# Segment mean over ten million sorted values: 90 rows of 875 in place of 98 rows of 800, looks from sums of probes, tables eight wide

## The chip, the core and the metric

The kernel runs on one core of a Trainium2 chip. The metric is the time of the whole program on the device in microseconds. The profile is one execution taken by the hardware profiler; its span runs from the first to the last instruction, and its own time is a little longer than the span.

## The reference: what is computed

```
data:        10,000,000 float32
segment_ids: 10,000,000 int64, sorted, 10,000 segments
sums[s]   = sum of data where segment_ids == s
counts[s] = number of elements where segment_ids == s
out[s]    = sums[s] / max(counts[s], 1)
```

The ids are sorted draws, so a segment is a run of about 1,000 neighbouring elements; in the fixed draw the shortest has 886 elements and the longest 1,136.

## The kernel before, in words

**Tiling.** Each of the 128 partitions owns D = 78,125 neighbouring elements, cut into NR = 98 rows of L = 800 (the last has 525). A row of one partition holds at most one boundary between segments, because a segment is longer than a row. The kernel doesn't read all ids. It finds each boundary in two looks.

**First look.** *Probes* are every S = 160th id, five to a row, one packet of 8 bytes each; `load_probes` (L153) loads them on SP's queue in 20 groups of four or five rows. `first_look` (L230 to L285) works on VectorE on one group: ten small operations compare the probes of a row with the first, add up how many are equal (`jc`), work out the place of the interval that holds the boundary (`ST`, `pos`, `IDX`) and a constant for the second look (`QQ`), and the boundary count of the row (`BT`) and its complement (`NB`). A row without exactly one boundary gets an index beyond the array.

**Second look.** `gather` (L287) is an indirect DMA on POOL's queue for each row; it fetches W = 159 ids for every partition into one of RING = 28 slots of `GT`, and nothing for partitions whose index is out of bounds. `add_ids` (L298) adds them on ScalarE; since the ids take only two values, the sum tells where the boundary is. `second_look` (L304) subtracts it from `QQ` and gives `KK`, the boundary's place within the row.

**Data.** `load_data` (L157) brings two rows a tile, 800 KB in a DMA of SP's queue, into 18 buffers. `total` (L310) sums a row on ScalarE into `T`. `split` (L316, the instruction at L319) sums on VectorE what lies ahead of the boundary: a ramp in PSUM is compared with `KK`, multiplied by the data and summed into `A`. `T - A` belongs to the next segment (`B`).

**Putting segments together.** A segment can start in one row and end in a later one, or in the next partition. `counts` (L521) carries the places of boundaries through rows by a scan and takes reciprocals of the lengths; `sums` (L560) does so for the partial sums (`FF`). `extend` (L372) shifts the first E = 24 rows of every partition to the partition below by a matmul, and `ext_rows` (L579) handles these. `select`, `table` (L633, L640) move results from row order to segment order: `windows` (L368) lets four neighbouring outputs look at the same twelve rows, compares keys with the output's number (`sel`), multiplies by the results and adds up (`tab`). `place` (L654, its second call on POOL) moves each partition's table to its place among the 79 outputs of a partition, by thirteen shifts (`shf`). The last outputs aren't taken from the table: `pick` (L672) prepares weights from the last rows, two wide operations of it on POOL, and `all_but_last` and `finish` (L696, L710) use them when the last sums are there. `check`, `check_late` and `verdict` (L450 to L519) make sure that the windows hold; if not, `general_path` computes everything in another way.

**Order.** It is written by hand. The loop over rows at the end issues, for each row r, loads up to X_DATA = 26 rows ahead and probes 13 further, `add_ids` of row r + 6, then `total` and `split` of row r, then whatever `put` has hung behind that row: looks 11 rows ahead of their group, `counts`, `sums`, `table` and so on at rows chosen by hand. Each engine and each DMA queue takes its instructions in this order and waits for what it needs.

Of the kernel before, what the change touches and what calls it, by code (L numbers as in the profile page):

```python
# [9 lines left out]
FP32 = mybir.dt.float32  # L10
BF16 = mybir.dt.bfloat16
I32 = mybir.dt.int32
# [7 lines left out]
L = 800  # L20
S = 160
K = L // S
NR = 98
LAST = D - (NR - 1) * L
W = S - 1
E = 24
NX = NR + E
BIG = float(1 << 24)
GROUPS = [4] + [5] * 18 + [4]
X_PROBE = 13  # L30
X_DATA = 26
X_LOOK = 11
X_SUM = 6
RING = 28
# [3 lines left out]
NT1 = 92  # L38
R1 = 84
R2 = NR + 4  # L40
C1 = 50
# [71 lines left out]
def kernel(  # L113
# [30 lines left out]
    NPR = (D + S - 1) // S  # L144

# [20 lines left out]

    wb_i = cpool.tile([P, NR], I32, name="wb_i")
    wb = cpool.tile([P, NR], FP32, name="wb")
    nc.gpsimd.iota(wb_i, pattern=[[L, NR]], base=-W, channel_multiplier=D)  # L169
# [3 lines left out]
    nc.gpsimd.iota(i_i, pattern=[[1, L]], base=0, channel_multiplier=0)  # L173
# [3 lines left out]
    nc.gpsimd.iota(rp_i[:, 0:NR], pattern=[[L, NR]], base=0, channel_multiplier=0)  # L177
    nc.gpsimd.iota(rp_i[:, NR:NX], pattern=[[L, E]], base=D, channel_multiplier=0)
# [3 lines left out]
    nc.gpsimd.iota(ur_i, pattern=[[1, NX]], base=0, channel_multiplier=0)  # L182
    nc.vector.tensor_scalar(out=ur, in0=ur_i, scalar1=-1.625, scalar2=None, op0=ALU.add)
# [24 lines left out]
    jj_i = cpool.tile([P, NT1], I32, name="jj_i")  # L208
    jj = cpool.tile([P, NT1], FP32, name="jj")
    nc.gpsimd.iota(jj_i, pattern=[[1, NT1]], base=0, channel_multiplier=0)  # L210
# [3 lines left out]
    PAD = 2  # L214
    q5 = cpool.tile([P, 5, NX + PAD], FP32, name="q5")
    nc.vector.memset(q5, 0.0)
    V, BT, KK, A, B = (q5[:, i, PAD:] for i in range(5))
    vend = cpool.tile([P, 1], FP32, name="vend")
    ST = cpool.tile([P, NR], FP32, name="ST")
    IDX = cpool.tile([P, NR], I32, name="IDX")  # L220
    QQ = cpool.tile([P, NR], FP32, name="QQ")
    GS = cpool.tile([P, NR], FP32, name="GS")
    T = cpool.tile([P, NR], FP32, name="T")
    NB = cpool.tile([P, NX], FP32, name="NB")
    GT = gpool.tile([P, RING, W], I64, name="GT")
    gt32 = GT.bitcast(I32)
# [3 lines left out]
    def first_look(g):  # L230

        a, b = bounds[g], bounds[g + 1]
        n = b - a
        eq = fpool.tile([P, n, K - 1], FP32, name="eq", bufs=3)
        jc = fpool.tile([P, n], FP32, name="jc", bufs=3)
        pos = fpool.tile([P, n], FP32, name="pos", bufs=3)
        last = b == NR

        def s1():
            if last:  # L240
                nc.vector.tensor_copy(out=pr32[:, NR - 1, 2 * (K - 1) : 2 * K], in_=snt32)
                nc.vector.tensor_copy(out=vend, in_=snt32[:, 0:1])
                nc.vector.tensor_copy(out=V[:, NR : NR + 1], in_=snt32[:, 0:1])
            in1b, in0b = bass.broadcast_tensor_aps(pr32[:, a:b, 0:1], pr32[:, a:b, 2 : 2 * K : 2])
            nc.vector.tensor_tensor(out=eq, in0=in0b, in1=in1b, op=ALU.is_equal)  # L245
            e = b if last else b + 1
            nc.vector.tensor_copy(out=V[:, a:e], in_=pr32[:, a:e, 0])  # L247

        def s2():
            nc.vector.tensor_reduce(out=jc, in_=eq, axis=AX.X, op=ALU.add)  # L250
            nc.vector.tensor_sub(out=BT[:, a:b], in0=V[:, a + 1 : b + 1], in1=V[:, a:b])  # L251

        def s3():
            nc.vector.tensor_scalar(  # L254
                out=ST[:, a:b], in0=jc, scalar1=float(S), scalar2=float(1 + W),
                op0=ALU.mult, op1=ALU.add,
            )
            nc.vector.tensor_scalar(  # L258
                out=NB[:, a:b], in0=BT[:, a:b], scalar1=1.0, scalar2=None, op0=ALU.not_equal
            )  # L260
            if last:
                nc.vector.tensor_scalar(
                    out=ST[:, NR - 1 : NR], in0=ST[:, NR - 1 : NR], scalar1=float(LAST), scalar2=None,
                    op0=ALU.min,
                )

        def s4():
            nc.vector.tensor_add(out=pos, in0=ST[:, a:b], in1=wb[:, a:b])  # L268
            nc.vector.scalar_tensor_tensor(  # L269
                out=QQ[:, a:b], in0=V[:, a:b], scalar=float(W), in1=ST[:, a:b],  # L270
                op0=ALU.mult, op1=ALU.add,
            )

        def s5():
            nc.vector.scalar_tensor_tensor(  # L275
                out=IDX[:, a:b], in0=NB[:, a:b], scalar=BIG, in1=pos, op0=ALU.mult, op1=ALU.add
            )

            nc.vector.scalar_tensor_tensor(  # L279
                out=QQ[:, a:b], in0=NB[:, a:b], scalar=-64.0 * BIG, in1=QQ[:, a:b], op0=ALU.mult,  # L280
                op1=ALU.add,
            )
            gather(g)

        return [s1, s2, s3, s4, s5]  # L285
# [12 lines left out]
    def add_ids(r):  # L298
        nc.scalar.activation(  # L299
            out=junk_a[:, 0:W], in_=gt32[:, r % RING, 0 : 2 * W : 2], func=ACT.Relu,  # L300
            accum_out=GS[:, r : r + 1],
        )

    def second_look(a, b):  # L304
        def s1():
            nc.vector.tensor_sub(out=KK[:, a:b], in0=QQ[:, a:b], in1=GS[:, a:b])  # L306

        return [s1]
# [23 lines left out]
    CS = cpool.tile([P, R2 + 1], FP32, name="CS")  # L332
    CX = cpool.tile([P, E + 1], FP32, name="CX")
# [3 lines left out]
    FF = cpool.tile([P, NX], FP32, name="FF")  # L337
    RF = cpool.tile([P, NX + PAD], FP32, name="RF")
    sel = cpool.tile([P, NT1 // 4, 4, 12], FP32, name="sel")
    tab = cpool.tile([P, NT1], FP32, name="tab")  # L340
    shf = cpool.tile([P, NO, ND], FP32, name="shf")
    KL = cpool.tile([P, R2 - R1], FP32, name="KL")
    pk = cpool.tile([P, NO - C1, R2 - R1], FP32, name="pk")
# [6 lines left out]
    nc.vector.memset(CS[:, 0:1], 0.0)  # L350
    nc.vector.memset(CX[:, 0:1], 0.0)
# [3 lines left out]
    MID = 68  # L355
    NBAD = 2 * (NR - MID) + 2
    bad0 = cpool.tile([P, 2 * (MID + E) + 5], FP32, name="bad0")
    bad = cpool.tile([P, NBAD], FP32, name="bad")
    vx = cpool.tile([P, 1], FP32, name="vx")
    bads = cpool.tile([P, 1], FP32, name="bads")  # L360
# [4 lines left out]
    def view(ap, dims):  # L365
        return bass.AP(ap.tensor, ap.offset, [list(ap.ap[0])] + dims)

    def windows(ap, m0, m1):  # L368

        return view(ap[:, 5 * m0 : 5 * m0 + 1], [[5, m1 - m0], [0, 4], [1, 12]])  # L370

    def extend():  # L372

        def s1():
            nc.vector.tensor_sub(out=B[:, 0:E], in0=T[:, 0:E], in1=A[:, 0:E])

# [23 lines left out]
    def keys(a, b):  # L400
        def s1():
            if a == 0:
                nc.vector.tensor_add(out=base1, in0=V[:, 0:1], in1=pin)

        def s2():
            nc.vector.tensor_scalar(
                out=KEY[:, PAD + a : PAD + b], in0=V[:, a:b], scalar1=base1[:, 0:1], scalar2=None,
                op0=ALU.subtract,
            )
            if a == 0:  # L410
                nc.vector.tensor_sub(out=delta, in0=sp, in1=base1)

        def s3():
            if a == 0:
# [6 lines left out]
    j1 = cpool.tile([P, NX], FP32, name="j1")  # L421
# [417 lines left out]
```

## Time and profile before

| | |
|---|---|
| time, median of 5 runs | 195.54 us (194.1 to 197.33) |
| time of the profiled execution | 195.72 us |
| its span | 194.0 us |
| VectorE (DVE) busy | 148.5 us, 77% of the span, 551 instructions |
| ScalarE (ACT) busy | 138.2 us, 71%, 393 instructions |
| POOL busy | 104.9 us, 54%, 117 instructions |
| `split`, L319 | 98 instructions, 102.3 us, mean 1,044 ns |
| `total`, L314 | 98 instructions, 85.0 us, mean 867 ns |
| `add_ids`, L299 | 98 instructions, 33.9 us, mean 346 ns |
| gathers, L289 | 98 instructions, 98.0 us, mean 1,000 ns |
| DMA | 53.40 MB in 75,141 packets, 65,601 of them under 512 B |

How to read it: the page gives each engine's busy time, then the span in 40 slices (a digit is the busy share in tenths), then the DMA queues with packets, MB and the share that their packets took of 16 engines' span, then the chain that ended last and the costliest groups of instructions. An answer of order in time gives start, duration, engine, line, operation and the tiles, with the idle time before it and what ended that. VectorE is DVE there, ScalarE ACT, SyncE SP; the queue of an engine has a q behind its name.

### The profile page before, as it was taken

Reading aid. Unit: us, or ns where it says so; the run is one execution under the profiler, and the core shown is the slowest. Engines: PE = TensorE matmul, PEld = TensorE weight load, DVE = VectorE, ACT = ScalarE, POOL = GpSimd, SP = SyncE. Lnnn points to the kernel's source line nnn. Section 1 sums busy time; section 2 is a strip of 40 time slices with the busy share of each in tenths; the row PEclk is TensorE's granted clock in tenths of the full one; section 3 lists DMA queues with packets and bytes.
Section 4 is the critical chain, followed back from the end, with each engine's and each line's share of the span. In section 5 each row is a group of like instructions: output and inputs, shape, how many; then the busy total and the mean of one; then the engine's idle time right before and its main releaser. Section 6 shows DMA issues by size and latency. Waiting matters only on the chain.

```text
span 194.0 us, 1611 instructions
## 1 busy us (share of the span) xinstructions
PE 1.6 (1%) x6; PEld 1.4 (1%) x6; DVE 148.5 (77%) x551; ACT 138.2 (71%) x393; POOL 104.9 (54%) x117
## 2 busy tenths in 40 slices
PE   0000000000000100000000000000000000001000
PEld 0000000000001000000000000000000000001000
DVE  6533596988694939596797949797998688999991
ACT  0221798999997869596869868687867697987800
POOL 5487765766657372846546472847275654762000
DMA  5999999999999999999999999899999999993000
GB/s 63 135 168 350 280 401 228 303 349 353 293 250 393 244 337 216 408 212 376 279 380 245 271 360 296 258 247 408 236 361 273 396 266 413 402 397 153 2 0 10
DMA packets 75141, 53.40 MB, mean 275 GB/s; under 512 B 65601, under 2 KB 65684, under 8 KB 75127
## 3 DMA queue, kind: packets, MB, share of 16 engines
q1 hardware_dynamic: 70251, 40.54, 74.5%
q0 software_dynamic: 4704, 12.74, 22.6%
q14 instruction: 14, 0.11, 0.2%
q10 hardware_dynamic: 172, 0.00, 0.1%
HBM read 56.46 MB, written 0.04 MB: 291 GB/s over the span
## 4 chain that ended last, share of the span: by engine, by line
DMA 41%; SPq 29%; DVE 13%; issue 9%; POOL 3%; ACT 2%; POOLq 0%; ACTq 0%; DVEq 0%
DMA data_t<-in_data_dram 34%; SPq L161 24%; DMA GT<-in_segment_ids_dram,IDX 8%; DVE junk_v L319 6%; SPq L153 5%; POOL GT L289 3%; ACT junk_a L314 1%; ACT junk_a L299 1%; DVE FF L572 1%; DVE most L706 0%; DVE pk L684 0%; DVE add L701 0%; DVE sel L642 0%; DVE sel L628 0%; DVE tab L647 0%
## 5 line engine op out<-in xcount | busy, mean ns | idle before, releaser
L289 POOL DMA_INDIRECT GT<-in_segment_ids_dram,IDX x98 | 98.0, 1000 | 67.1 <-ACT junk_a L299 24.1
L319 DVE SCALAR_TENSOR_TENSOR junk_v<-iota,q,data_t 128x800 bf16<-128x800 f32 x98 | 102.3, 1044 | 25.5 <-DMA data_t<-in_data_dram 23.7
L314 ACT ACTIVATE junk_a<-data_t 128x800 bf16<-128x800 f32 x98 | 85.0, 867 | 14.3 <-DMA data_t<-in_data_dram 11.3
L299 ACT ACTIVATE junk_a<-GT 128x159 bf16<-128x159 int32 x98 | 33.9, 346 | 23.8 <-DMA GT<-in_segment_ids_dram,IDX 19.3
L299 ACT ACTIVATION_READ_ACCUMULATOR junk_a<-GT 128x1 f32 x98 | 18.3, 187 | 0.0
L314 ACT ACTIVATION_READ_ACCUMULATOR junk_a<-data_t 128x1 f32 x98 | 18.3, 186 | 0.0
L306 DVE TENSOR_TENSOR q<-QQ,GS 128x5 f32<-128x5 f32 (+1 forms) x20 | 3.2, 160 | 7.3 <-ACT junk_a L299 3.9
L319 DVE DVE_READ_ACCUMULATOR junk_v<-iota,q,data_t 128x1 f32 x98 | 8.1, 82 | 0.0
L245 DVE TENSOR_TENSOR eq<-pr 128x20 f32<-128x20 int32 (+1 forms) x20 | 3.4, 172 | 4.6 <-issue 2.5
L299 ACT ACT_TABLE_LOAD x1 | 1.3, 1283 | 7.6 <-DMA data_t<-in_data_dram 7.6
L254 DVE TENSOR_SCALAR ST<-jc 128x5 f32<-128x5 f32 (+1 forms) x20 | 3.8, 192 | 0.0
L268 DVE TENSOR_TENSOR pos<-ST,wb 128x5 f32<-128x5 f32 (+1 forms) x20 | 3.3, 166 | 0.5 <-DVE NB L258 0.4
L275 DVE SCALAR_TENSOR_TENSOR IDX<-NB,pos 128x5 int32<-128x5 f32 (+1 forms) x20 | 3.3, 164 | 0.5 <-DVE QQ L269 0.5
L250 DVE TENSOR_REDUCE jc<-eq 128x5 f32<-128x20 f32 (+1 forms) x20 | 3.5, 175 | 0.0
L258 DVE TENSOR_SCALAR NB<-q 128x5 f32<-128x5 f32 (+1 forms) x20 | 3.5, 174 | 0.0
L247 DVE CAST q<-pr 128x6 f32<-128x6 int32 (+2 forms) x20 | 3.3, 166 | 0.0
L279 DVE SCALAR_TENSOR_TENSOR QQ<-NB,QQ 128x5 f32<-128x5 f32 (+1 forms) x20 | 3.2, 162 | 0.0
L269 DVE SCALAR_TENSOR_TENSOR QQ<-q,ST 128x5 f32<-128x5 f32 (+1 forms) x20 | 3.1, 157 | 0.0
L251 DVE TENSOR_TENSOR q<-q 128x5 f32<-128x5 f32 (+1 forms) x20 | 3.1, 155 | 0.0
L657 POOL TENSOR_TENSOR shf<-tab,dm 128x559 f32<-128x559 f32 x1 | 1.3, 1331 | 1.9 <-DVE tab L647 1.9
L647 DVE TENSOR_REDUCE tab<-sel 128x32 f32<-128x384 f32 (+2 forms) x3 | 1.6, 531 | 0.0
L170 DVE CAST wb<-wb_i 128x98 f32<-128x98 int32 x1 | 0.8, 783 | 1.1 <-POOL wb_i L169 1.1
(107 smaller groups left out, 42.1 us busy)
## 6 DMA issues: line engine op xcount, KB each, us to landing
data_t<-in_data_dram SPq DMA_DIRECT2D x48, 800.0 KB
GT<-in_segment_ids_dram,IDX POOLq DMA_INDIRECT x98
pr<-in_segment_ids_dram SPq DMA_DIRECT2D x18, 25.0 KB
data_t<-in_data_dram SPq DMA_DIRECT2D x1, 400.0 KB
data_t<-in_data_dram SPq DMA_DIRECT2D x1, 262.5 KB
out_dram<-OUT SPq DMA_DIRECT2D x1, 36.6 KB
pr<-in_segment_ids_dram SPq DMA_DIRECT2D x1, 21.0 KB
pr<-in_segment_ids_dram SPq DMA_DIRECT2D x1, 18.0 KB
```

What stands on the lines that cost most here:

```text
L153: nc.sync.dma_start(out=pr_flat[:, a:b], in_=ids_p[:, a * S : (b - 1) * S + 1 : S])
L161: nc.sync.dma_start(out=d[:, 0 : c - a], in_=data_p[:, a:c])
L245: nc.vector.tensor_tensor(out=eq, in0=in0b, in1=in1b, op=ALU.is_equal)
L247: nc.vector.tensor_copy(out=V[:, a:e], in_=pr32[:, a:e, 0])
L250: nc.vector.tensor_reduce(out=jc, in_=eq, axis=AX.X, op=ALU.add)
L254: nc.vector.tensor_scalar(out=ST[:, a:b], in0=jc, scalar1=float(S), scalar2=float(1 + W), op0=ALU.mult, op1=ALU.add,)
L258: nc.vector.tensor_scalar(out=NB[:, a:b], in0=BT[:, a:b], scalar1=1.0, scalar2=None, op0=ALU.not_equal)
L268: nc.vector.tensor_add(out=pos, in0=ST[:, a:b], in1=wb[:, a:b])
L289: nc.gpsimd.indirect_dma_start(out=GT[:, r % RING, :], out_offset=None, in_=ids2d[:], in_offset=bass.IndirectOffsetOnAxis(ap=IDX[:, r : r ...
L299: nc.scalar.activation(out=junk_a[:, 0:W], in_=gt32[:, r % RING, 0 : 2 * W : 2], func=ACT.Relu, accum_out=GS[:, r : r + 1],)
L314: nc.scalar.activation(out=junk_a[:, 0:n], in_=d, func=ACT.Copy, accum_out=t)
L319: nc.vector.scalar_tensor_tensor(out=junk_v[:, 0:n], in0=iota[:, 0:n], scalar=KK[:, r : r + 1], in1=d, op0=ALU.is_lt, op1=ALU.mult, accum_ ...
```

## The change

- **Rows and probes.** Rows of 875 elements, 90 of them, the last with 250; a probe every 175 elements, still five to a row (447 in place of 489 for a partition). Groups are 15 of six rows. Gathers fetch 175 ids. The ring of `GT` has 20 slots, the tables for the next partition E = 20 rows. Looks go 12 rows ahead, probes 14, `add_ids` 7.
- **Looks.** `first_look` adds up the row's probes (`SG`) and takes `ST = 5 * next row's first id - SG`; with one boundary this is the number of probes behind it. Zero, no boundary, is sent out of bounds by adding 2^18 before the multiplication by 175. `YY` replaces `QQ`. `BT` and `NB` are made later, for many rows at once, in `keys`. `add_ids` uses a plain copy and no longer a ReLU, and ScalarE fills all of `GT` with zeros at the start.
- **Counts and sums.** The scans run on maxima and on sums with the multiplier of the row, so that fewer operations are needed; a row without a boundary is pushed far below by `-512 * FAR`.
- **Tables.** `windows` is eight rows wide and slides by one row for each output, seven outputs to eight rows. The part of the table that comes from the next partition has its own table (`tax`), placed early. All of `place` runs on VectorE; `pick` gets a third wide operation on POOL.
- **Check.** One check of all rows behind rows 74 to 76, its verdict behind rows 77 and 78.

```diff
-L = 800
-S = 160
+L = 875
+S = 175
 K = L // S
-NR = 98
+NR = 90
 LAST = D - (NR - 1) * L
-W = S - 1
-E = 24
+TAIL = LAST - S
+W = S
+E = 20
 NX = NR + E
-BIG = float(1 << 24)
-GROUPS = [4] + [5] * 18 + [4]
-X_PROBE = 13
+FAR = float(1 << 18)
+GROUPS = [6] * 15
+X_PROBE = 14
 X_DATA = 26
-X_LOOK = 11
-X_SUM = 6
-RING = 28
+X_LOOK = 12
+X_SUM = 7
+RING = 20
 NO = 79
 SHIFT = 6
 ND = 2 * SHIFT + 1
-NT1 = 92
-R1 = 84
+NT1 = 91
+M1 = 10
+R1 = 8 * M1 - 2
 R2 = NR + 4
-C1 = 50
+C1 = 51
...
+    GT = gpool.tile([P, RING, W], I64, name="GT")
+    gt32 = GT.bitcast(I32)
+
+    def view(ap, dims):
+        return bass.AP(ap.tensor, ap.offset, [list(ap.ap[0])] + dims)
+
+    nc.scalar.activation(
+        out=gt32[:, :, 0 : 2 * W : 2], in_=view(q5[:, 0, 0:1], [[0, RING], [0, W]]), func=ACT.Copy
...
-        pos = fpool.tile([P, n], FP32, name="pos", bufs=3)
+        far = fpool.tile([P, n], FP32, name="far", bufs=3)
         last = b == NR
 
         def s1():
+            v = nc.vector
             if last:
-                nc.vector.tensor_copy(out=pr32[:, NR - 1, 2 * (K - 1) : 2 * K], in_=snt32)
-                nc.vector.tensor_copy(out=vend, in_=snt32[:, 0:1])
-                nc.vector.tensor_copy(out=V[:, NR : NR + 1], in_=snt32[:, 0:1])
-            in1b, in0b = bass.broadcast_tensor_aps(pr32[:, a:b, 0:1], pr32[:, a:b, 2 : 2 * K : 2])
-            nc.vector.tensor_tensor(out=eq, in0=in0b, in1=in1b, op=ALU.is_equal)
-            e = b if last else b + 1
-            nc.vector.tensor_copy(out=V[:, a:e], in_=pr32[:, a:e, 0])
-
-        def s2():
-            nc.vector.tensor_reduce(out=jc, in_=eq, axis=AX.X, op=ALU.add)
-            nc.vector.tensor_sub(out=BT[:, a:b], in0=V[:, a + 1 : b + 1], in1=V[:, a:b])
-
-        def s3():
-            nc.vector.tensor_scalar(
-                out=ST[:, a:b], in0=jc, scalar1=float(S), scalar2=float(1 + W),
-                op0=ALU.mult, op1=ALU.add,
-            )
-            nc.vector.tensor_scalar(
-                out=NB[:, a:b], in0=BT[:, a:b], scalar1=1.0, scalar2=None, op0=ALU.not_equal
+                m = NR * K + 1 - NPR
+                v.tensor_copy(
+                    out=pr_flat.bitcast(I32)[:, 2 * NPR : 2 * (NPR + m)].rearrange("p (a b) -> p a b", b=2),
+                    in_=view(snt32[:, 0:1], [[0, m], [1, 2]]),
+                )
+            v.tensor_reduce(out=SG[:, a:b], in_=pr32[:, a:b, 0 : 2 * K : 2], axis=AX.X, op=ALU.add)
+            v.scalar_tensor_tensor(
+                out=ST[:, a:b], in0=VI[:, a + 1 : b + 1], scalar=float(K), in1=SG[:, a:b],
+                op0=ALU.mult, op1=ALU.subtract,
+            )
+            v.tensor_scalar(out=far, in0=ST[:, a:b], scalar1=0.0, scalar2=FAR, op0=ALU.is_equal, op1=ALU.mult)
+            v.tensor_add(out=ST[:, a:b], in0=ST[:, a:b], in1=far)
+            for c, d, w in [(a, b - 1, S), (b - 1, b, TAIL)] if last else [(a, b, S)]:
+                v.scalar_tensor_tensor(
+                    out=IDX[:, c:d], in0=ST[:, c:d], scalar=float(w), in1=wb[:, c:d], op0=ALU.mult, op1=ALU.add
+                )
+            v.scalar_tensor_tensor(
+                out=YY[:, a:b], in0=ST[:, a:b], scalar=float(K + 1), in1=SG[:, a:b], op0=ALU.mult, op1=ALU.add
             )
             if last:
-                nc.vector.tensor_scalar(
-                    out=ST[:, NR - 1 : NR], in0=ST[:, NR - 1 : NR], scalar1=float(LAST), scalar2=None,
-                    op0=ALU.min,
+                v.tensor_scalar(
+                    out=tl, in0=ST[:, NR - 1 : NR], scalar1=-1.0, scalar2=float(TAIL - S),
+                    op0=ALU.add, op1=ALU.mult,
                 )
-
-        def s4():
-            nc.vector.tensor_add(out=pos, in0=ST[:, a:b], in1=wb[:, a:b])
-            nc.vector.scalar_tensor_tensor(
-                out=QQ[:, a:b], in0=V[:, a:b], scalar=float(W), in1=ST[:, a:b],
-                op0=ALU.mult, op1=ALU.add,
-            )
-
-        def s5():
-            nc.vector.scalar_tensor_tensor(
-                out=IDX[:, a:b], in0=NB[:, a:b], scalar=BIG, in1=pos, op0=ALU.mult, op1=ALU.add
-            )
-
-            nc.vector.scalar_tensor_tensor(
-                out=QQ[:, a:b], in0=NB[:, a:b], scalar=-64.0 * BIG, in1=QQ[:, a:b], op0=ALU.mult,
-                op1=ALU.add,
-            )
             gather(g)
 
-        return [s1, s2, s3, s4, s5]
...
-            out=junk_a[:, 0:W], in_=gt32[:, r % RING, 0 : 2 * W : 2], func=ACT.Relu,
+            out=junk_a[:, 0:W], in_=gt32[:, r % RING, 0 : 2 * W : 2], func=ACT.Copy,
...
-            nc.vector.tensor_sub(out=KK[:, a:b], in0=QQ[:, a:b], in1=GS[:, a:b])
+            nc.vector.scalar_tensor_tensor(
+                out=KK[:, a:b], in0=YY[:, a:b], scalar=float(S // K), in1=GS[:, a:b],
+                op0=ALU.mult, op1=ALU.subtract,
...
+    nc.gpsimd.memset(tab, 0.0)
+    nc.gpsimd.memset(tax, 0.0)
+    nc.gpsimd.memset(shf[:, :, ND : ND + 1], 0.0)
+    nc.gpsimd.memset(add, 0.0)
...
-        return view(ap[:, 5 * m0 : 5 * m0 + 1], [[5, m1 - m0], [0, 4], [1, 12]])
+        return view(ap[:, 8 * m0 : 8 * m0 + 1], [[8, m1 - m0], [1, 7], [1, 8]])
...
+    def edges(a, b):
+        nc.vector.tensor_sub(out=BT[:, a:b], in0=VI[:, a + 1 : b + 1], in1=VI[:, a:b])
...
-    def counts(a, b):
+    def counts(a, b, mask=True):
 
 
         n = b - a
         ps = fpool.tile([P, n], FP32, name="ps")
-        bp = fpool.tile([P, n], FP32, name="bp")
         ct = fpool.tile([P, n], FP32, name="ct")
 
         def s1():
-            nc.vector.tensor_add(out=ps, in0=rp[:, a:b], in1=KK[:, a:b])
-
-        def s2():
-            nc.vector.tensor_mul(out=bp, in0=ps, in1=BT[:, a:b])
+            nc.vector.scalar_tensor_tensor(
+                out=ps, in0=NB[:, a:b], scalar=-512.0 * FAR, in1=KK[:, a:b], op0=ALU.mult, op1=ALU.add
+            )
+
+        def s2():
+            nc.vector.tensor_add(out=ps, in0=ps, in1=rp[:, a:b])
 
         def s3():
             nc.vector.tensor_tensor_scan(
-                out=PS[:, a + 1 : b + 1], data0=NB[:, a:b], data1=bp, initial=PS[:, a : a + 1],
-                op0=ALU.mult, op1=ALU.add,
+                out=PS[:, a + 1 : b + 1], data0=ps, data1=ps, initial=PS[:, a : a + 1],
+                op0=ALU.max, op1=ALU.max,
             )
 
         def s4():
             nc.vector.tensor_sub(out=ct, in0=ps, in1=PS[:, a:b])
 
         def s5():
-            nc.vector.tensor_scalar(out=ct, in0=ct, scalar1=1.0, scalar2=None, op0=ALU.max)
+            nc.vector.reciprocal(out=RB[:, a:b], in_=ct)
 
         def s6():
-            nc.vector.reciprocal(out=ct, in_=ct)
-
-        def s7():
-            c = min(b, NR)
-            nc.vector.tensor_mul(out=RB[:, a:c], in0=ct[:, 0 : c - a], in1=BT[:, a:c])
-            if b > NR:
-                nc.vector.tensor_mul(
-                    out=RB[:, NR:b], in0=ct[:, NR - a : n], in1=MX[:, 0 : b - NR]
-                )
-
-        return [s1, s2, s3, s4, s5, s6, s7]
+            nc.vector.tensor_mul(out=RB[:, a:b], in0=RB[:, a:b], in1=BT[:, a:b])
+
+        return [s1, s2, s3, s4, s5] + ([s6] if mask else [])
 
     def sums(a, b, weigh=True, upto=NR):
         def s1():
...
+            nc.vector.tensor_add(out=XX[:, a:b], in0=A[:, a:b], in1=q5[:, 4, PAD + a - 1 : PAD + b - 1])
+
+        def s3():
             nc.vector.tensor_tensor_scan(
-                out=CS[:, a + 1 : b + 1], data0=NB[:, a:b], data1=B[:, a:b], initial=CS[:, a : a + 1],
+                out=FF[:, a:b], data0=NBP[:, a:b], data1=XX[:, a:b], initial=FFP[:, a : a + 1],
                 op0=ALU.mult, op1=ALU.add,
             )
-
-        def s3():
-            nc.vector.tensor_add(out=FF[:, a:b], in0=A[:, a:b], in1=CS[:, a:b])
...
+    def place(c0, c1, t, outs):
+        def s1():
+            n = c1 - c0
+            nc.vector.tensor_tensor(
+                out=shf[:, c0:c1, 0:ND], in0=view(t[:, c0 : c0 + 1], [[1, n], [1, ND]]),
+                in1=view(dm[:, 0:1], [[0, n], [1, ND]]), op=ALU.mult,
+            )
+
+        def s2():
+            for a, b, d, o in outs:
+                nc.vector.tensor_reduce(out=o, in_=shf[:, a:b, 0:d], axis=AX.X, op=ALU.add)
+
+        return [s1, s2]
+
...
-                  view(jj[:, C1 : C1 + 1], [[1, n], [0, m]]))
+                out=pk, in0=view(KL[:, 0:1], [[0, n], [1, m]]), in1=view(jj[:, C1 : C1 + 1], [[1, n], [0, m]]),
+                op=ALU.subtract,
+            )
+            e.tensor_scalar(out=pk, in0=pk, scalar1=0.0, scalar2=None, op0=ALU.is_equal)
+            e.tensor_copy(out=BM[:, 0 : NR - R1], in_=BT[:, R1:NR])
+            e.tensor_copy(out=BM[:, NR - R1 : m], in_=MX[:, 0 : R2 - NR])
+            e.tensor_tensor(out=pk, in0=pk, in1=view(BM[:, 0:1], [[0, n], [1, m]]), op=ALU.mult)
...
             after[r + i // every].append(f)
 
     for g in range(HEAD):
-        for f in first_look(g):
-            after[-1].append(f)
+        after[-1] += first_look(g)
     after[-1] += second_look(0, GROUPS[0])
     for a, b in zip(bounds[1:], bounds[2:]):
         put(a - 1, second_look(a, b))
     for g in range(HEAD, NG):
-        put(max(bounds[g] - X_LOOK, 0), first_look(g), 5)
-
-    v, g = nc.vector, nc.gpsimd
+        put(max(bounds[g] - X_LOOK, 0), first_look(g))
+
     verdict_reg = []
-    put(26, extend())
-    put(48 - X_LOOK, keys(0, 48))
-    put(36, ext_rows())
-    put(45, select(0, 8, v))
-    put(46, counts(0, 48))
-    put(52, sums(0, 48) + table(0, 8, v))
-    put(57, keys(48, MID)[1:] + keys(NR, NX)[1:2])
-    put(58, select(8, 12, v))
-    put(64, counts(48, 66), 2)
-    put(67, sums(48, 66) + table(8, 12, v) + place(0, 36, v), 2)
-    put(60, check(), 2)
-    last_look = bounds[NG - 1] - X_LOOK
-    put(last_look + 1, keys(MID, NX)[1:2] + check_late(), 3)
-    put(last_look + 1, pick()[:1])
-    put(last_look + 2, select(12, NT1 // 4, v))
-    put(R1, counts(66, R1), 4)
-    put(R1 + 2, sums(66, R1), 4)
-    t, p = table(12, NT1 // 4, v), place(36, NO, g)
-    put(R1 + 3, t + p[:1])
-    put(R1 + 6, p[1:])
-    put(R1 + 1, [lambda: nc.sync.dma_start(out=out2d[0:SHIFT, :].rearrange("n u -> u n"), in_=tab[0:1, 0:SHIFT])])
-    put(R1 + 4, verdict())
-    after[R1 + 6].append(lambda: verdict_reg.append(nc.values_load(badi[0:1, 0:1], min_val=0, max_val=1)))
-    put(NR - 4, counts(R1, R2), 4)
-    put(NR - 3, pick()[1:], 2)
+    m = R2 - R1
+    T1, CE = 7 * M1, 7 * M1 - ND + 1
+    Q1, Q2 = 44, 68
+    H1, H2 = 5, 8
+    assert 8 * (H1 - 1) + 12 <= Q1 and 8 * (H2 - 1) + 12 <= Q2
+    O2 = 7 * H2 - ND + 1
+    put(E + 1, extend())
+    put(E + 6, ext_rows())
+    put(38, keys(0, 48))
+    put(41, keys(NR, NX)[1:2] + select(M1, NT1 // 7))
+    t = table(M1, NT1 // 7, tax)
+    p = place(CE, NO, tax, [(CE, T1, ND, shf[:, CE:T1, ND]), (T1, NO, ND, add[:, T1 - C1 :, m])])
+    put(43, t + p)
+    put(41, counts(0, Q1), 2)
+    put(45, sums(0, Q1) + select(0, H1) + table(0, H1, tab), 2)
+    put(60, [lambda: nc.sync.dma_start(out=out2d[0:SHIFT, :].rearrange("n u -> u n"), in_=tab[0:1, 0:SHIFT])])
+    put(62, keys(48, R1)[1:], 2)
+    put(65, counts(Q1, Q2), 2)
+    put(Q2, sums(Q1, Q2) + select(H1, H2) + table(H1, H2, tab), 2)
+    put(72, place(0, O2, tab, [(0, O2, ND + 1, OUT[:, 0:O2])]))
+    look = bounds[NG - 1] - X_LOOK
+    put(look + 1, keys(R1, NR)[1:], 2)
+    put(look + 1, pick()[:1])
+    put(look + 2, check())
+    put(look + 5, verdict(), 1)
+    after[look + 7].append(lambda: verdict_reg.append(nc.values_load(badi[0:1, 0:1], min_val=0, max_val=1)))
+    put(74, counts(Q2, R1), 2)
+    put(R1, sums(Q2, R1) + select(H2, M1) + table(H2, M1, tab), 2)
+    c = min(NO, T1)
+    assert O2 <= C1
+    put(R1 + 4, place(O2, c, tab, [(O2, C1, ND + 1, OUT[:, O2:C1]), (C1, c, ND + 1, add[:, 0 : c - C1, m])]))
+    put(NR - 6, counts(R1, R2, False), 3)
+    put(NR - 4, pick()[1:], 2)
     put(NR - 2, all_but_last(), 5)
     assert max(after) <= NR - 1
 
```

## Prediction

> **What bounds the kernel now.** I read the busy slices and the queue shares of the page first, then the windows before and after 160 us, then VectorE's (DVE's) order of time around 160 us and at the end.
>
> ```profile
> DVE  6533596988694939596797949797998688999991
> ACT  0221798999997869596869868687867697987800
> POOL 5487765766657372846546472847275654762000
> DMA  5999999999999999999999999899999999993000
> ...
> q1 hardware_dynamic: 70251, 40.54, 74.5%
> q0 software_dynamic: 4704, 12.74, 22.6%
> ```
>
> The DMA engines are at 90% or more from 5 to 175 us, while ScalarE, POOL and VectorE have gaps; at the end it is VectorE that is full and DMA that is empty. q1 carries data and probes, q0 the gathers.
>
> ```profile
> core 0: us, PE busy (x) PEld busy (x) DVE busy (x) ACT busy (x) POOL busy (x), PEclk, DMA share, GB/s
> 0.00:160.00 160.00, 0.99 (x4) 0.93 (x4) 119.93 (x460) 117.52 (x339) 94.20 (x107) 1.00 1.07 292
> 160.00:194.00 34.00, 0.59 (x2) 0.50 (x2) 28.53 (x91) 20.64 (x56) 10.71 (x11) 1.00 0.50 196
> ```
>
> Before 160 us the packets' time is 1.07 of all 16 engines (packets of two queues overlap); after it VectorE is busy 28.5 of the 30 us until the outputs go.
>
> ```profile
> 160.48 1.05 DVE L319 SCALAR_TENSOR_TENSOR junk_v<-iota,q,data_t 128x800 bf16<-128x800 f32 x1 [0.98 <-DMA data_t<-in_data_dram]
> ...
> 170.32 1.09 POOL L630 TENSOR_TENSOR pk<-KL,jj 128x522 f32<-128x522 f32 x1
> 170.53 0.92 DVE L572 TENSOR_TENSOR FF<-q,CS 128x18 f32<-128x18 f32 x1
> 171.50 1.55 POOL L631 TENSOR_SCALAR pk<-pk 128x522 f32<-128x522 f32 x1
> ...
> 188.77 0.76 DVE L319 SCALAR_TENSOR_TENSOR junk_v<-iota,q,data_t 128x525 bf16<-128x525 f32 x1
> 189.45 0.08 DVE L319 DVE_READ_ACCUMULATOR junk_v<-iota,q,data_t 128x1 f32 x1
> 189.45 0.24 DVE L712 SCALAR_TENSOR_TENSOR most<-wq,T,most 128x29 f32<-128x29 f32 x1
> 189.73 0.25 DVE L715 SCALAR_TENSOR_TENSOR OUT<-wp,q,most 128x29 f32<-128x29 f32 x1
> 190.00 1.48 SPq L719 DMA_DIRECT2D out_dram<-OUT  x2
> ```
>
> The split of row 82 at 160.48 us is the last instruction of VectorE that waits for data. From there VectorE runs without a gap to 190.00. So the time is the landing of the tile that decides (160.0), plus VectorE's work from its row on (160.48 to 190.00, 29.5 us), plus 4.0 us of output, plus 1.7 us outside the span (195.72 - 194.0). That execution lies 0.2 us above the median of the runs (195.54). A gain has to come from an earlier landing near 64,000 elements of each partition, or from less VectorE work behind it.
>
> **DMA work: two changes that nearly cancel.** The single packets in the trace: 62,592 probes of 8 B at 10.1 ns (632 us of engine time), data 1,666 us (a 6,400 B packet 247 ns in the median, 3,200 B 131), gathers 701 us; divided by 16: 39.5, 104 and 43.8 us. After: 447 probes per partition for 489, so 57,216 packets, -54/16 = -3.4 us. Data: the same bytes in 512 fewer packets; a straight line through 131 and 247 ns leaves 15 ns a packet, -0.5 us. Gathers: rows without a boundary are skipped before and after, and with 10,000 boundaries, each in a row of its own in both grids (counted in the reference's draw), 10,000 gathers move bytes, 1,272 B each before and 1,400 B after: +1.28 MB. At the median pace of a 5,088 B packet (208 ns) that is 3.3 us, at the mean pace of q0 (12.74 MB in 701 us) 4.4 us. Whole sum: -0.6 to +0.5 us, nothing.
>
> A rule of the Trainium skill would make more of it: DMA: Bandwidth & Descriptors, section Anatomy of one DMA, gives each DMA from POOL's queue some 2.0 us of fixed cost. Eight gathers fewer would save 16 us by it. The row says otherwise: the engines are at 9 all through, so the fixed part of one gather lies under the packets of others, and only packets count. I take nothing.
>
> **When the deciding tile lands.** The whole sum is not what decides; VectorE meets the data at about 64,750 elements (end of row 73 of 875). Before, 64,000 had landed at 152.4 us and 65,600 at 156.1 (last packets of tiles 39 and 40), so 64,750 at 154.1. By then q1 has done 38.0 of its 39.5 us of probes before, and after the change all 36.1 (the last probes go out ahead of tile 35): -1.9. Gathers: those issued 6 us earlier have landed (gather of row 84 issued 148.28, read 155.3). Before that is 84 of 98, 30.9 to 37.5 us of DMA time at the two paces; after, looks run 12 rows of 875 ahead in groups of six, deeper in elements than 11 rows of 800, so 80 of 90: 35.2 to 42.8 us, +4.3 to +5.3. Data -0.4. Together +2.0 to +3.0, divided by the overlap of 1.08: +1.9 to +2.8. I take +2.3: landing at 156.4.
>
> **VectorE behind it.** Prices from its own starts: rows of 800 follow each other at 1.095 us (17.64, 18.73, 19.83); 1,047 ns at 800 and 756 at 525 elements give 1.05 ns each, so 1.17 us for 875, and the last row (250 for 525 elements) costs 0.39 us to its accumulator. A small operation costs 0.08 us if it doesn't need the one before it and 0.21 if it does (182.03, 182.25, 182.46), a scan or reciprocal about 0.30; wide ones add 1.04 ns per element (sel, 528: 0.62).
> - Looks: ten operations for 5 rows took 0.98 us (100.77 to 101.75), as two chains that fill each other's latency. The new seven are nearly one chain (sum, ST, far, ST, IDX): 0.08 + 4 x 0.21 + 2 x 0.08 = 1.1 us for 6 rows. Per row 0.18 for 0.20: most of the saved instructions are paid back in latency.
> - From row 72, behind the rows: 72 last look and table placing (572 wide) 2.06; 73 reduce 616 and keys 1.07; 74 to 76 the check, now whole and here, with counts 2.40; 77 to 79 verdict and sums 1.14; 80 to 83 table 112 wide, placing 338 on VectorE, its reduces 1.91; 84 to 87 counts and pick (448 wide) 1.75; 88 the last sums (448 and 476 wide) 1.95. Sum 12.3.
> - Rows 72 to 88: 17 x 1.17 = 19.9. Last row and the two closing operations 0.39 + 0.28 + 0.27 = 0.94. Together 33.1 us.
>
> The kernel before has 31.7 us from row 80 (157.34 to 190.00 without the wait of 0.98) for 14,125 elements; here it is 33.1 for 15,125. Per element 2.24 and 2.19 ns: a gain of 0.7 us, no more.
>
> **POOL beside VectorE.** FF (18 elements) took 0.92 us at 170.53 while POOL ran pk, against 0.18 elsewhere: a stall of 0.74. pick on POOL now has three operations of 448 for two of 522; placing (1.33 us at 559) leaves POOL. The SBUF — State Buffer page, section Who interferes with whom, says that a VectorE instruction with two SBUF inputs is shut out for the whole of a POOL instruction that reads SBUF, or the other way round. Scaled by width the three take some 0.95 + 1.35 + 0.95 = 3.25 us; by the rule up to that is lost, by the row 0.74 once. The split's ramp lies in PSUM and is safe, so only the small operations between can be hit: I charge 0.5.
>
> **Hidden parts.** The fill of GT on ScalarE: 3,500 elements at 0.82 ns (867 ns at 800, 642 at 525) plus 0.2, 3.1 us; done near 5 us, before the first indices (6.6). POOL's four new memsets, under 1 us, end about there too; the first gather slips 0.25 us. The first group has six rows for four, so row 0's split waits for two more gathers: 20.5 for 17.64. VectorE later waits 23.7 us for data, which covers it; uncovered it would cost 2.9. ScalarE: 1.46 us per row of 800, 1.54 per row of 875, against a landing every 1.93; ahead. Its new early wait for the verdict (behind row 79) has the last two id sums behind it, needed at row 83 of VectorE, about 3 us later. SP passes one small output between its last data loads; the table it reads is old by then.
>
> **Sum.** 156.4 + 0.4 (landing to start) + 33.1 + 0.5 = 190.4; + 4.0 + 1.7 = 196.1; less the 0.2 to the median, about **196.0 us**. The same sum from row 64 gives an end 1 us earlier, so no other tile decides clearly.
>
> **Rivals.** (1) Faster: the gathers' extra bytes ride in the overlap and the landing stays at 154.1, with no stall of POOL. Then VectorE ends at 187.6 and other tiles limit: from row 64, at 143 + 47, less the 1 to 2 us that the landing also gains there, about 188; time 193. For it: overlap of 1.07 is what two queues make. Against: data falls to 236 GB/s in windows with many probes, so the engines have no spare time. (2) Slower: POOL's three pick operations shut VectorE out each time, 3.25 for 0.5: 198.8. It decides from two full stalls on, 1.5 us over my sum. For it: the row of 0.92; against: one of several chances before. (3) Slower: the late start of row 0 isn't made up, and gathers come to ScalarE late all along: 196.0 + 2.9 = 198.9. Against it the 23.7 us of waits for data. (4) The new windows don't hold for this draw and the general path runs: worked out from the inputs, the farthest key lies 20.5 from its window's middle for an allowed 21.75; excluded.
>
> **How the numbers follow.** A measurement of this kernel can't tell much under 1%. My forecast (within 193.6 to 197.5) 0.41; faster, rival 1, 0.27, since each DMA term was charged near its upper half; slower 0.32: rival 2 0.19, rival 3 with landings at the upper bound 0.13. The range of 193.0 to 199.0 takes in rivals 1 to 3 at their worked values and leaves out some 2 in 10; the forecast's own is 194.5 to 197.5.
>
> **What would show it.** Right: q0 near 24 to 25% with 14.0 MB and q1 near 57,000 probes; VectorE's last wait for data near row 70 to 74 at 155 to 158 us; 33 to 34 us from there to the output; look chains of 1.1 us. Wrong: a last wait for data beyond 165 us (then DMA decides to the end), several VectorE operations of 0.9 us and more around 165 to 170 us (rival 2), or splits that wait for id sums (rival 3).

## The result, and the profile after

| | before | after |
|---|---|---|
| time, median | 196.14 us (79 runs, 194.1 to 199.85) | 194.45 us (42 runs, 192.94 to 196.16) |
| ratio after / before | | 0.9932, 95% interval 0.9917 to 0.9948 |
| time of the profiled execution, its span | 195.72, 194.0 us | 195.33, 193.6 us |
| VectorE (DVE) busy, instructions | 148.5 us, 551 | 138.5 us, 421 |
| VectorE's waits for data | 23.7 us | 29.5 us |

The kernel is 0.7% faster, about 1.3 us; the forecast was no change (196.0 us). VectorE was relieved of 10 us of work, and the time fell by 1.3. The medians are of all runs; the ratios leave out runs that lie over 1.5% above the fastest of the same kernel. The profiled execution after lies 0.9 us above the median of its runs, that of before 0.4 us below its own (over all 79), so the two traces show less of a difference (0.4 us) than the medians do; this matters below.

The page of the kernel after, the same rows as in the prediction (busy tenths of the span in 40 slices; queues with packets, MB, share of 16 engines):

```profile
DVE  6330765974875849759299897738849689999991
ACT  8112569999996949769397784879849589499900
POOL 5578774747466272754807437373662826770000
DMA  6999999999999999999999999999999999995000
...
q1 hardware_dynamic: 64219, 40.50, 71.8%
q0 software_dynamic: 5760, 14.01, 22.3%
```

The shape is that of before: the DMA engines are full to 175 us, and VectorE at the end. The windows of the kernel after (duration, then busy time of each engine, granted clock, DMA share, GB/s):

```profile
core 0: us, PE busy (x) PEld busy (x) DVE busy (x) ACT busy (x) POOL busy (x), PEclk, DMA share, GB/s
0.00:160.00 160.00, 0.98 (x4) 0.93 (x4) 109.63 (x329) 116.39 (x311) 87.75 (x104) 1.00 1.03 299
160.00:194.00 34.00, 0.59 (x2) 0.50 (x2) 28.83 (x93) 20.50 (x52) 10.36 (x13) 1.00 0.51 200
```

Here is where the 10 us went. All of them (119.93 to 109.63) left the stretch ahead of 160 us, in which VectorE waits for the DMA engines anyway; behind it VectorE is busy 28.83 us, for 28.53 before. Work taken from an engine that waits comes back as waiting: VectorE's waits for data grew by 5.8 us, and those for probes and sums of ids by 3.7 (11.8 to 15.5).

VectorE's order of time in the kernel after (start, duration, instruction, idle time before it), at its last wait, at the one stall beside POOL, and at the end:

```profile
157.98 1.13 DVE L324 SCALAR_TENSOR_TENSOR junk_v<-iota,q,data_t 128x875 bf16<-128x875 f32 x1 [0.65 <-DMA data_t<-in_data_dram]
...
161.01 1.13 DVE L324 SCALAR_TENSOR_TENSOR junk_v<-iota,q,data_t 128x875 bf16<-128x875 f32 x1
...
169.30 0.95 POOL L638 TENSOR_TENSOR pk<-KL,jj 128x448 f32<-128x448 f32 x1
...
169.72 0.55 DVE L306 SCALAR_TENSOR_TENSOR q<-YY,GS 128x6 f32<-128x6 f32 x1
...
188.61 0.47 DVE L324 SCALAR_TENSOR_TENSOR junk_v<-iota,q,data_t 128x250 bf16<-128x250 f32 x1
189.00 0.08 DVE L324 DVE_READ_ACCUMULATOR junk_v<-iota,q,data_t 128x1 f32 x1
189.00 0.24 DVE L681 SCALAR_TENSOR_TENSOR most<-wq,T,most 128x28 f32<-128x28 f32 x1
...
189.55 1.07 SPq L688 DMA_DIRECT2D out_dram<-OUT  x1
```

The last wait for data is that of row 72 (element 63,000), at 157.98 us. From there to the output's issue at 189.55 are 31.57 us: the tail. The tail before was 29.52 us from element 65,600. Counted from the same element the kernel before needs about 33.5 us (from three quarters of row 78, whose split starts at 153.99 and is followed 2.02 us later, to 190.00, without the 0.98 of waiting), or 33.2 if the 0.28 us of idle time ahead of row 80 is waiting for data too: the new tail is some 1.7 to 1.9 us shorter.

### The profile page after: what moved, and what is told of

It is laid out like the page before. It is cut to its first block, busy times and chain, and to the rows that moved or that the text cites. A ratio compares the mean times of both kernels' runs of the same rounds, so it can differ in the third digit from the quotient of the medians.

```text
span 193.6 us, 1420 instructions
## 1 busy us (share of the span) xinstructions
PE 1.6 (1%) x6; PEld 1.4 (1%) x6; DVE 138.5 (72%) x421; ACT 136.9 (71%) x362; POOL 98.1 (51%) x117
## 3 DMA queue, kind: packets, MB, share of 16 engines
q0 software_dynamic: 5760, 14.01, 22.3%
## 4 chain that ended last, share of the span: by engine, by line
DMA 39%; SPq 35%; DVE 14%; issue 7%; ACT 2%; POOL 1%; DVEq 0%; POOLq 0%; ACTq 0%
DMA data_t<-in_data_dram 38%; SPq L164 30%; DVE junk_v L324 7%; SPq L156 4%; ACT junk_a L319 1%; DMA GT<-in_segment_ids_dram,IDX 1%; POOL GT L289 1%; ACT junk_a L299 1%; DVE shf L615 1%; DVE OUT L622 0%; DVE most L675 0%; DVE add L670 0%; DVE q L306 0%; DVE pk L648 0%; DVE FFP L533 0%
## 5 line engine op out<-in xcount | busy, mean ns | idle before, releaser
L289 POOL DMA_INDIRECT GT<-in_segment_ids_dram,IDX x90 | 90.2, 1002 | 72.5 <-ACT junk_a L319 38.1
L324 DVE SCALAR_TENSOR_TENSOR junk_v<-iota,q,data_t 128x875 bf16<-128x875 f32 x90 | 100.7, 1119 | 30.7 <-DMA data_t<-in_data_dram 29.5
L319 ACT ACTIVATE junk_a<-data_t 128x875 bf16<-128x875 f32 x90 | 83.7, 930 | 23.6 <-DMA data_t<-in_data_dram 21.0
L299 ACT ACTIVATE junk_a<-GT 128x175 bf16<-128x175 int32 x90 | 32.4, 360 | 22.7 <-DMA GT<-in_segment_ids_dram,IDX 20.0
L306 DVE SCALAR_TENSOR_TENSOR q<-YY,GS 128x6 f32<-128x6 f32 x15 | 2.8, 186 | 9.9 <-ACT junk_a L299 6.7
L264 DVE TENSOR_REDUCE SG<-pr 128x6 f32<-128x30 int32 x15 | 2.7, 180 | 5.5 <-DMA pr<-in_segment_ids_dram 5.5
L180 ACT ACTIVATE GT<-q 128x3500 int32<-128x3500 f32 x1 | 3.3, 3312 | 0.0
L269 DVE TENSOR_SCALAR far<-ST 128x6 f32<-128x6 f32 x15 | 2.7, 180 | 0.5
L272 DVE SCALAR_TENSOR_TENSOR IDX<-ST,wb 128x6 int32<-128x6 f32 (+2 forms) x16 | 2.6, 165 | 0.5
L265 DVE SCALAR_TENSOR_TENSOR ST<-pr,SG 128x6 f32<-128x6 int32 x15 | 2.5, 166 | 0.5
```

What stands on the lines that cost most here:

```text
L180: nc.scalar.activation(out=gt32[:, :, 0 : 2 * W : 2], in_=view(q5[:, 0, 0:1], [[0, RING], [0, W]]), func=ACT.Copy)
L264: v.tensor_reduce(out=SG[:, a:b], in_=pr32[:, a:b, 0 : 2 * K : 2], axis=AX.X, op=ALU.add)
L265: v.scalar_tensor_tensor(out=ST[:, a:b], in0=VI[:, a + 1 : b + 1], scalar=float(K), in1=SG[:, a:b], op0=ALU.mult, op1=ALU.subtract,)
L269: v.tensor_scalar(out=far, in0=ST[:, a:b], scalar1=0.0, scalar2=FAR, op0=ALU.is_equal, op1=ALU.mult)
L272: v.scalar_tensor_tensor(out=IDX[:, c:d], in0=ST[:, c:d], scalar=float(w), in1=wb[:, c:d], op0=ALU.mult, op1=ALU.add)
L289: nc.gpsimd.indirect_dma_start(out=GT[:, r % RING, :], out_offset=None, in_=ids2d[:], in_offset=bass.IndirectOffsetOnAxis(ap=IDX[:, r : r ...
```

## The experiments

Two ideas were to be told apart. The theory: the end is the landing of the tile near 64,000 elements plus VectorE's tail behind it, and the forecast priced that tail too high, because a row of 1.17 us holds a gap that a small operation behind the row fills for nothing. The rival: the tail's length doesn't count, and what changed the time lies on the DMA side alone (bytes, packets, and how far ahead they are asked for). The four kernels ran on one chip, where the kernel before took 195.01 us in the median of 23 runs. The kernel after was not among them; by its ratio it would be 193.7 there.

**Without the check (e1_no_check).** Does a piece of work behind the last wait cost its full length?

```diff
+    nc.gpsimd.memset(bad, 0.0)
...
-    put(look + 2, check())
```

> The changed kernel without the twelve operations of the check behind rows 74 to 76 (left out: the check that the windows hold; its flags are zeros). In the changed kernel's trace these operations take 0.39 + 0.44 + 0.57 = 1.40 us of VectorE's line behind the deciding tile. Theory (VectorE's work behind the deciding tile sets the end): 1.2 to 1.5 us faster than the changed kernel, about 193.1 us. Rival (the gain and the end come from the DMA engines' reduced work, VectorE has room at the end): no change, 194.4 us within 0.4.

Measured: 193.55 us in the median of 6 runs, ratio to before 0.989 (0.983 to 0.995). The expected 1.2 to 1.5 us are not seen in the times: by the ratios this kernel is 0.8 us faster than the kernel after, with intervals that overlap, and the two kernels below that compute everything took 193.6 and 193.46 us on the same chip. So the rival's "no change" is not excluded by the times; the traces have to tell. Last wait at 157.82 us, that is where the kernel after has it (157.98), and the output is issued at 187.99: a tail of 30.17 us for 31.57, 1.40 less. The table has the time from the split of one row to that of the next:

| row | after | no check | solo operations |
|---|---|---|---|
| 72 | 3.03 | 3.03 | 3.03 |
| 73 | 2.17 | 2.18 | 2.18 |
| 74 | 1.72 | 1.33 | 1.72 |
| 75 | 1.83 | 1.40 | 1.83 |
| 76 | 1.95 | 1.38 | 1.94 |
| 77 | 1.81 | 1.42 | 1.81 |
| 78 | 1.41 | 1.61 | 1.41 |
| 79 | 1.42 | 1.40 | 1.43 |
| 80 | 1.55 | 1.73 | 1.54 |
| 81 to 88 | 13.74 | 13.74 | 13.74 |

Rows 74 to 76 lost 1.39 us with the check. The other three differences cancel: row 77 lost 0.39, rows 78 and 80 got 0.20 and 0.18. They are one stall in two places. In the kernel after it is `KK` at 169.72 (the fence above: 0.55 us beside POOL's `pk`); without the check `KK` comes 1.5 us earlier and has gone by when `pk` starts, and two later operations are hit, by the first and by the third of POOL's wide operations:

```profile
168.19 0.16 DVE L306 SCALAR_TENSOR_TENSOR q<-YY,GS 128x6 f32<-128x6 f32 x1
...
169.07 0.95 POOL L639 TENSOR_TENSOR pk<-KL,jj 128x448 f32<-128x448 f32 x1
...
169.68 0.37 DVE L528 TENSOR_TENSOR q<-T,q 128x10 f32<-128x10 f32 x1
...
171.81 1.13 POOL L646 TENSOR_TENSOR pk<-pk,BM 128x448 f32<-128x448 f32 x1
...
172.62 0.46 DVE L592 TENSOR_TENSOR sel<-KEY,jj 128x112 f32<-128x112 f32 x1
```

So in these two traces, whose last waits lie 0.16 us apart, the tail sets the end one for one: 1.40 us less of tail, 1.57 us between the two outputs. That the median time follows it is not shown. POOL's three wide operations (0.95, 1.34 and 1.13 us) cost VectorE 0.39 us in one kernel and 0.38 in the other.

**A solo operation behind rows that have none (e4_solo_ops).** This measures the disputed price by itself. Thirty rows that have nothing hung behind them get a copy of six elements that nothing reads:

```diff
+    solo = cpool.tile([P, 6], FP32, name="solo")
...
+            if not after[r]:
+                nc.vector.tensor_copy(out=solo, in_=rp[:, 0:6])
```

> The changed kernel with one added operation on VectorE (a copy of six elements to a tile that nobody reads) behind each row that has nothing else behind it. Theory (two splits in direct succession have a gap of about 0.12 us between them, and one small operation fits into it): rows whose data is there already follow each other at 1.17 to 1.19 us as without it. Price list of the forecast (a row's 1.17 plus 0.08 for the operation): 1.25 us. Both: the time does not change within 0.5 us, since these rows lie ahead of the deciding tile.

Measured: 193.6 us, ratio 0.992 (0.988 to 0.996). VectorE's order of time in the kernel after, without such a copy, and below it in that kernel:

```profile
20.63 1.13 DVE L324 SCALAR_TENSOR_TENSOR junk_v<-iota,q,data_t 128x875 bf16<-128x875 f32 x1
21.69 0.08 DVE L324 DVE_READ_ACCUMULATOR junk_v<-iota,q,data_t 128x1 f32 x1
21.81 1.13 DVE L324 SCALAR_TENSOR_TENSOR junk_v<-iota,q,data_t 128x875 bf16<-128x875 f32 x1
```

```profile
53.30 1.12 DVE L324 SCALAR_TENSOR_TENSOR junk_v<-iota,q,data_t 128x875 bf16<-128x875 f32 x1
54.35 0.08 DVE L324 DVE_READ_ACCUMULATOR junk_v<-iota,q,data_t 128x1 f32 x1
54.35 0.17 DVE L785 COPY solo<-rp 128x6 f32<-128x6 f32 x1
54.46 1.13 DVE L324 SCALAR_TENSOR_TENSOR junk_v<-iota,q,data_t 128x875 bf16<-128x875 f32 x1
55.52 0.08 DVE L324 DVE_READ_ACCUMULATOR junk_v<-iota,q,data_t 128x1 f32 x1
55.52 0.17 DVE L785 COPY solo<-rp 128x6 f32<-128x6 f32 x1
55.64 1.13 DVE L324 SCALAR_TENSOR_TENSOR junk_v<-iota,q,data_t 128x875 bf16<-128x875 f32 x1
```

The splits follow each other at 1.16 and 1.18 us with the copy between them. Without one they do so at 1.18 and 1.17 (20.63, 21.81, 22.98 in the kernel after). From the accumulator's start to the next split pass 0.11 to 0.12 us, whether the copy stands there or not: a small operation behind a row that needs nothing from its split is free. The forecast's list, 1.17 for the row and 0.08 for the operation, would have given 1.25.

This run shows a second thing. Its tail is that of the kernel after in every row (the table), yet its profiled execution took 192.4 us, 2.9 less. The tile of rows 72 and 73 landed at 153.8 us here and at 156.5 there, and the last wait for data came at row 70, 151.72 us, two rows ahead of where it is in the kernel after. The queues carry the same packets in both but for one. The tail stays within 0.1 us (31.57 and 31.65), and the landing moves by 2.7.

**Half of each gather (e2_short_gather).** Are the gathers' bytes on the path, and at what price?

```diff
-                out=GT[:, r % RING, :],
+                out=GT[:, r % RING, 0:88],
```

> The changed kernel with gathers of 88 ids for 175 (left out: the second half of each gathered interval, so boundaries are misplaced): 7.0 MB of gathers for 14.0, some 21 us less packet time for each engine over the whole run, about 17 us of it ahead of row 72. Theory (up to row 72 the DMA engines decide): 8 to 17 us faster than the changed kernel, 178 to 187 us, until VectorE's and ScalarE's own work is the limit. Rival (the landing of data is set by the eight loads in flight or by buffers, not by the packets' work): less than 2 us faster.

Measured: 178.52 us, ratio 0.913 (0.907 to 0.918), as the theory expected, and far from the rival's 2 us. The page of that kernel:

```profile
DVE  7421591979889797797699999769499799999990
...
DMA  5999999999999999999999999999998999980000
...
q1 hardware_dynamic: 64219, 40.50, 83.4%
q0 software_dynamic: 4320, 7.05, 13.9%
```

6.96 MB less took 15 us from the time (193.7 to 178.5), 2.2 us per MB, and the whole chart has moved to the left: the tile of rows 72 and 73 lands at 140.0 us, and from row 72 to the output are 31.55 us, the same tail. The number of gathers is the same, 90, so what the gathers move is on the path: bytes, and packets with them (5,760 to 4,320). What a gather costs beside its bytes was not varied.

**The leads of before (e3_less_lead).** Is the landing later because looks, probes and sums run further ahead?

```diff
-X_PROBE = 14
+X_PROBE = 13
-X_LOOK = 12
-X_SUM = 7
+X_LOOK = 11
+X_SUM = 6
```

> The changed kernel with the leads of the kernel before: looks 11 rows ahead, id sums 6, probes 13 (for 12, 7, 14). Theory (probes and gathers that run further ahead put the deciding tile back by some 2 us): one row less of lead brings gathers of one row (0.48 us) and probes of one row (0.4 us) back behind it, the last wait for data moves from 158.0 to about 157.2 us, and the time falls by 0.5 to 0.9 us. Rival (the lead hides the gathers' latency, and ScalarE now comes late with the sums of ids): slower by 0.5 us or more, with waits of the second look for ScalarE.

Measured: 193.46 us, ratio 0.990 (0.987 to 0.994). The last wait for data, expected at 157.2 us, is at 155.72, 2.3 us earlier than in the kernel after; this can't be put down to the leads, since the landing moves as much between two executions with equal leads (the run with solo operations). The ratio's interval overlaps that of the kernel after. Rows of VectorE's waits in this kernel (us in total, times, longest):

```profile
DVE junk_v L324 <- DMA data_t<-in_data_dram: 26.3, 14, 3.5
DVE q L306 <- ACT junk_a L299: 10.5, 4, 6.6
...
DVE q L306 <- issue: 0.3, 1, 0.3
```

and in the kernel after:

```profile
DVE junk_v L324 <- DMA data_t<-in_data_dram: 29.5, 19, 3.7
DVE q L306 <- ACT junk_a L299: 6.7, 2, 5.7
...
DVE q L306 <- issue: 3.3, 1, 3.3
```

`KK` (L306) waits 10.8 us in whole for 10.0, the splits 3.2 us less for data: the shorter leads bring no new wait of size. Whether they gain anything is inconclusive; by the intervals at most some 1.5 us (0.9948 less 0.9871, of 195 us). POOL cost more here. A subtraction of ten elements that took 0.15 us in the kernel after (171.61) was issued just behind the start of `pk`:

```profile
168.81 0.95 POOL L638 TENSOR_TENSOR pk<-KL,jj 128x448 f32<-128x448 f32 x1
168.91 0.87 DVE L527 TENSOR_TENSOR q<-T,q 128x10 f32<-128x10 f32 x1
```

## Why the prediction was wrong

**The step that failed: "VectorE behind it".** It gave 33.1 us plus 0.5 for POOL's stall, 33.6; measured 31.57. Rows and last row are right: 17 x 1.17 = 19.9 and 0.94. The operations behind the rows were to take 12.3 us; from the splits' starts they take 10.74 (188.61 - 157.98 - 19.89), and the stall is in this already (0.39 in row 77). So 12.8 was forecast for 10.74, 2.05 us too much. Nearly all of it is the gap: each of the 17 rows has something hung behind it, and each was charged for the 0.12 us that its first operation fills. The forecast's own groups show it (us behind the rows, measured without the stall):

| rows | priced | measured |
|---|---|---|
| 72 | 2.06 | 1.86 |
| 73 | 1.07 | 1.01 |
| 74 to 76 | 2.40 | 1.99 |
| 77 to 79 | 1.14 | 0.74 |
| 80 to 83 | 1.91 | 1.39 |
| 84 to 87 | 1.75 | 1.37 |
| 88 | 1.95 | 2.00 |

The groups of several rows were priced too high by 0.10 to 0.14 us a row. Row 88 was not: its first operation needs the sum that the split has just written, starts 0.19 us behind the accumulator's read (186.49 and 186.68), and so can't use the gap. The other 16 rows at 0.12 make 1.9 us, and 1.93 is what the list is too long by.

Before, the tail was read off the trace whole and so carried no such error; only the kernel after was priced from a list. That made the gain of 2.24 to 2.19 ns per element too small: it is 31.57 us for 15,125 elements, 2.09 ns.

**From landing to start.** The tile landed at 156.5 us for a forecast 156.4, and the split that needs it started at 157.98 for 156.8: 1.5 us after the last packet, where 0.4 had been read off one row before (160.0 to 160.48). The same trace had longer ones just ahead of it: 1.1, 1.6 and 1.3 us at rows 76, 78 and 80. Three other runs have 1.0 to 1.3 (156.8 to 157.82, 154.4 to 155.72, and at most 153.8 to 154.85, where the split waited for nothing). With the tail this explains the profiled execution: 157.98 + 31.57 + 4.05 + 1.73 = 195.33 us. The prediction took the profile to lie 0.2 us above the median; after, it lies 0.9 above, and this is the other part of the miss (196.0 against 194.45: +1.2 - 2.05 - 0.7).

**The landing, 2.3 us later, is not confirmed.** 156.5 us in the profile after looks like a hit. The runs without the check and with solo operations, with practically the same DMA work, have 156.8 and 153.8. The spread is as large as the shift that was forecast. The sum behind the forecast didn't come true either: of the packets that had ended by that landing (154.1 us before, 156.5 after), probes took 4.0 us an engine less, for a forecast 1.9, and gathers 0.5 more, for 4.3 to 5.3, though they moved 1.5 MB more. (The 4.3 is itself off: at the pace that was named, 208 ns for 5,088 B, it is 3.9.) So the hit is luck. What the medians leave is worked out, not shown: a tail 1.7 to 1.9 us shorter and a time 1.3 us shorter leave 0.4 to 0.6 us of later landing.

**DMA work.** That gains and losses nearly cancel held in the whole (share ahead of 160 us 1.03 for 1.07, last data landed at 177.3 us for 176.7), but not term by term. Probes: 57,216 packets at 9.48 ns are 33.9 us an engine, 5.6 less than before, for a forecast 3.4. Gathers: 43.1 us for 14.01 MB (43.7 to 46.1 in three other runs), for 43.75 with 12.74 MB before, where 3.3 to 4.4 more were forecast; data 104.3 for 104.2. Packets' time fell by 6 us an engine, and in these two traces nothing landed earlier. It is no measure of the way's length where packets of two queues overlap: in the run with half gathers, probes grew from 9.5 to 12.1 ns each. At that run's 2.2 us per MB the gathers' 1.28 MB would be 2.8 us, an estimate, against the 3.4 that were forecast for the probes. What the saved probes alone are worth was not run.

**The fixed cost per DMA.** It was right not to take the rule of the Trainium skill (DMA: Bandwidth & Descriptors, section Anatomy of one DMA) of some 2.0 us for each as time that adds up: eight gathers fewer would have been 16 us by it, an estimate, and the whole change is 1.3. With 90 gathers kept and their bytes halved the time fell by 15, so bytes count; a smaller fixed part is not excluded.

**POOL beside VectorE.** 0.5 us charged, 0.39 measured, one stall, as chosen; that the sizes agree is luck. Rival 2, VectorE shut out for the whole of all three operations (the Trainium skill, SBUF — State Buffer, section Who interferes with whom, carried to its upper end), did not happen: 0.39, 0.38 and, with the shorter leads, 0.70 us of a possible 3.4. Yet the shutting out is real, one operation at a time. A small operation with two inputs from SBUF, issued while POOL's `TENSOR_TENSOR` `pk` ran, ended only 0.02 to 0.03 us behind it: `KK` at 170.27 and `pk` at 170.25, in the kernel without the check 170.05 and 170.02, with the shorter leads 169.78 and 169.76, before (`FF`) 171.44 and 171.41. What is lost is thus the rest of `pk` at that moment. POOL's `TENSOR_SCALAR` cost nothing: before, the multiplication of 528 elements at 172.54 us took 0.70 us inside the one of 1.55 us, as long as one of 522 with POOL idle (184.60).

The last look, behind row 72, and the placing of the table took 1.86 us for a priced 2.06.

**Hidden parts.** The fill of `GT` took 3.3 us (3.1), row 0's split started at 20.63 (20.5), and it was made up: the last wait of the second look ends at 40.16 us, so rival 3 is out. Rival 1 named a time (193) on the right side, by no stall and no later landing. There was a stall of 0.39 us; the landing stays open, and the 0.4 to 0.6 us worked out above lie nearer to its zero than to the forecast's 2.3. What it did not name is the tail, cheaper per element than priced.

**What stays open.** The size of the landing's shift, what moves the landing from one execution to another, why the times do not show the 1.40 us that the check took from the tail, and a version better than this. Moving the last look or the late table ahead of the last wait might cut the tail by what they take there (row 72 alone holds 1.86 us behind its split); this was not run, nor is any of the runs above that computes everything surely faster than the kernel after.

## What to carry to other kernels

An operation saved ahead of an engine's last wait buys waiting; before pricing an edit, find that wait and count only what lies behind it. Price a stretch of instructions by start-to-start differences of the same pattern (a row with one operation, a row with two), not by a bare row plus operations: the bare row contains a gap that the first of them fills, if it doesn't need that row's sum. And compare two traces stretch by stretch only as far as each repeats: here the tail did to 0.1 us where its instructions were the same, the landing to 3.

## What the runs showed of the hardware that was not expected

- The 0.12 us between an accumulating split's read of its accumulator and the next split is free room for one independent small operation (a copy of six elements: 1.16 to 1.18 us from split to split with and without it).
- A small VectorE operation with two inputs from SBUF, issued during a `TENSOR_TENSOR` of POOL, ended 0.02 to 0.03 us behind it (0.15 us became 0.87 at worst); during a `TENSOR_SCALAR` of POOL of 1.34 to 1.55 us none was held up.
- A gather's packets hold at most three pieces of 1,400 B here and held at most four of 1,272 B before: 5,760 packets of 14.01 MB took 43.1 us an engine, 4,704 of 12.74 MB 43.75, so 20.3 for 18.2 GB/s per engine. In three other runs of the same gathers it was 43.7 to 46.1 us, so the gain in pace is not sure.
- Packets of 8 bytes took 9.5 ns in the mean, and 12.1 ns in the run with half of each gather: the price of a packet is not fixed.
